# Four feed-forwards of an encoder: one ring for the weight sums, a shifted turn of the operand tiles, and the memory's squares on VectorE

## The chip, the cores and the metric

The kernel runs on one core of a Trainium2 chip. The metric is device time in microseconds (us), from runs on the chip. TensorE (PE in the profile) multiplies matrices, VectorE (DVE), ScalarE (ACT) and GpSimd (POOL) work element by element, and SyncE (SP) issues most DMAs. A DMA that adds to what lies at its destination is issued by POOL here ("accumulate").

## The reference

A two-layer encoder over 512 tokens of 1024 features, in float32. Each layer has a feed-forward, a mixer (attention), a cross attention to a memory of 256 tokens, and a second feed-forward:

```python
def rmsnorm(x, g):
    xf = x.astype(jnp.float32)
    y = xf * lax.rsqrt(jnp.mean(xf * xf, axis=-1, keepdims=True) + EPS)
    return (y * g.astype(jnp.float32)).astype(x.dtype)

def swiglu(x, wg, wu, wd):
    return (jax.nn.silu(x @ wg) * (x @ wu)) @ wd
...
    h = x
    for layer in range(DEPTH):
        g, wg, wu, wd = ffn1[layer]
        h = h + 0.5 * swiglu(rmsnorm(h, g), wg, wu, wd)
        mix_g, mix_params = mix[layer]
        if layer % 2 == 0:
            h = h + even_mixer(rmsnorm(h, mix_g), *mix_params, t5_bias, layer)
        else:
            h = h + odd_mixer(rmsnorm(h, mix_g), *mix_params)
        mg, sg, wq, wkv, qg, kg, wo = memx[layer]
        h = h + memory_xattn(rmsnorm(h, mg), rmsnorm(mem, sg), wq, wkv, qg, kg, wo)
        g, wg, wu, wd = ffn2[layer]
        h = h + 0.5 * swiglu(rmsnorm(h, g), wg, wu, wd)
```

The hidden width of a feed-forward is 2816, 22 blocks of 128.

## The kernel before, in words

The change touches the four feed-forwards, which run at about 0 to 348, 719 to 1038, 1038 to 1367 and 1697 to 2030 us of the profiled execution. Between them stand the mixers and the cross attentions.

**Split products.** A float32 matrix product is made of three products of rounded parts: each operand is split into a high part (ScalarE copies it, rounded) and a low part (VectorE subtracts the high part from it), and high x high, low x high and high x low are added in PSUM. `operand` (L541 high, L542 low) does this for weights. One "product" of a pair is 24 matmuls of 128x256 (18 in the first chunk of the down projection).

**Pairs.** The 22 hidden blocks go in eleven pairs. Pair 0 is plain (`plain_pair`, `plain_end`: there R, the tokens' norm factor, is transposed by TensorE at L418 and copied by VectorE at L419). Pairs 1 to 10 use seven products of quarters instead of eight, in Strassen's manner. For pair p, TensorE's order is: sum t1 and sum t2 (`sum_pair`), cross with w12 and cross t3 (`cross_pair`), then the opening product of pair p+1 with its w11 (`open_pair`), then lower and upper of pair p (`close_pair`). A weight quarter is fetched by SP (`fetch`, L550) into a tile; quarters that have to be added are added by POOL's accumulate. Two tiles hold such sums:

- s1 (in `sum_pair`): SP fetches a quarter, POOL accumulates another on top (L601); t1 multiplies it. Then VectorE subtracts w11 from it in place (L607), t2 multiplies that; last, `close_pair` replaces it by w12 minus it (L655), for upper. So s1 lives through a whole pair. Three buffers.
- s3 (in `cross_pair`): SP fetches a quarter, ScalarE negates it (L632), POOL accumulates another on top (L633); t3 multiplies it. One buffer.

Every operand's high and low parts go into a ring of two tiles (wh, wl), and each third time into tiles of their own (sh, sl); a counter f.n in `operand` decides the turn. The last block of the down projection (L835) also writes its weights into sh and sl.

**Down projection.** The hidden blocks go down in chunks of 6, 8 and 8 blocks. The first two go by seven products as well (`paired_down`, after pairs 3 and 7), with its own s1 (accumulate L760) and s3 (L778) from the same buffers; the last is plain.

**Memory.** In the first feed-forward, `mem_stats` also loads the eight blocks of the memory (128x256) in two lots of four, at pairs 2 and 3. ScalarE squares them, and GpSimd adds the squares (L260), at pairs 3 and 4; at pair 6 the norm factors are made of the sum.

**Order.** PE's order is the one in which the code is written. On the other engines a scheduler in the framework sets the order of instructions when the kernel is built, by its own estimates, by priorities (`high_priority`) and by the order demanded with `behind`; each engine then runs its list strictly in order, and so do SP's and POOL's DMA issues. `f.factored` is the copy of pair 0's norm factor on VectorE (L405).

Of the kernel before, what the change touches and what calls it, by code (L numbers as in the profile page):

```python
# [11 lines left out]
F32 = mybir.dt.float32  # L12
# [7 lines left out]
P = 128  # L20
S = 512
D = 1024
F = 2816
KB = D // P
FB = F // P
QB = S // P
NMEM = 256
# [43 lines left out]
CHUNKS = (6, 8, 8)  # L71
# [3 lines left out]

MEM_SQUARES, MEM_FACTOR = (3, 4), 6
LAMBDA_INIT = 0.8 - 0.6 * math.exp(0.0)
# [35 lines left out]
class Encoder:  # L113
# [205 lines left out]
    def ffn(self, pre):  # L319


        with ExitStack() as ctx:
            pool = lambda name: ctx.enter_context(self.tc.tile_pool(name=pre + name, bufs=1))
            f = self.f = SimpleNamespace(pre=pre, ctx=ctx, hp=pool("h"), tp=pool("t"), H={}, n=0, taken=None, own=False, low=None, gate=None, ahead=None, spread=None, macc=None,
                                        G=[])
# [5 lines left out]
            for p in range(1, FB // 2):  # L331
# [17 lines left out]
                else:  # L349
# [4 lines left out]
                    else:  # L354
                        gate()
                    if c in PAIRED and p == ends[c]:
                        self.paired_down(c)
                        c += 1
# [169 lines left out]

    def operand(self, t, own=None):

        nc, f = self.nc, self.f
        n = t.shape[-1]
        if own is None:
            own = f.n % 3 == 2
            f.n += 1
        if own:
            h, l = (x[:, :n] for x in self.own_tiles())
        else:
            h, l = [self.wp.tile([P, 1024 + WHOLE], F32R, name=name, tag=name, bufs=2)[:, o:o + n]
                    for name, o in (("wh", LINE), ("wl", LINE + STEP))]  # L540
        self.leading = nc.scalar.activation(h, t, AF.Copy)  # L541
        self.parted = nc.vector.tensor_sub(l, t, h.bitcast(F32))  # L542
        return h, l
# [50 lines left out]
    def sum_pair(self, pair):  # L594
# [3 lines left out]
        with self.tc.high_priority():  # L598
            pair.s = f.tp.tile([P, 1024], F32, name="s1", tag="s1", bufs=3)
            self.fetch(pair.s, p, 3, f.first)  # L600
            nc.gpsimd.dma_start(pair.s, self.quarter(p, 2), accum_op=OP.add)  # L601
            w = self.operand(pair.s)
        with self.tc.high_priority():
# [12 lines left out]
    def cross_pair(self, pair):  # L616
# [11 lines left out]
        with self.tc.high_priority():  # L628
            s = f.tp.tile([P, 1024], F32, name="s3", tag="s3", bufs=1)
            self.fetch(s, p, 2)  # L630
# [104 lines left out]
    def paired_down(self, c):  # L735
# [11 lines left out]
        for s in range(2):  # L747
# [9 lines left out]
            with self.tc.high_priority():  # L757
                t = f.tp.tile([P, 1024], F32, name="s1", tag="s1", bufs=3)[:, :n]
                self.fetch(t, p, 3)
# [14 lines left out]
            with self.tc.high_priority():  # L774
                v = f.tp.tile([P, 1024], F32, name="s3", tag="s3", bufs=1)[:, :n]
                self.fetch(v, p, 2)
# [647 lines left out]
    def mem_keys(self, pre, mp):  # L1424
# [14 lines left out]
        return kh, kl, vp  # L1439

    def mem_stats(self, p):

        nc, f = self.nc, self.f
        if p in MEM_SQUARES:
            with self.behind(self.leading):
                for m in f.mem:
                    f.macc = self.square(f.macc, m, NMEM)
        if p + 1 in MEM_SQUARES:
            n = KB // len(MEM_SQUARES)
            f.mem, loaded = [], self.loaded  # L1450
            for k in range(MEM_SQUARES.index(p + 1) * n, MEM_SQUARES.index(p + 1) * n + n):
                if k % 2 == 0:
                    two = f.hp.tile([P, S], F32, name="mem", tag="T", bufs=max(CHUNKS))
                m = two[:, k % 2 * NMEM:k % 2 * NMEM + NMEM]
                with self.behind(loaded):
                    nc.sync.dma_start(m, self.I["memT"][k * P:(k + 1) * P, :])
                f.mem.append(m)
        if p == MEM_FACTOR:
# [448 lines left out]
```

## Time and profile before

| what | value |
|---|---|
| median of three runs | 2031.19 us (2030.74 to 2033.74) |
| the profiled execution | 2032.02 us |
| its span, first to last instruction | 2030.2 us |
| TensorE's mean granted clock | 0.998 |
| busy: PE, DVE, ACT, POOL | 2008.5, 1597.6, 1278.1, 357.0 us |
| HBM read | 301.64 MB |

The profile names a group of instructions by line, engine, operation and tiles (out<-in). A helper records many operations, so one line such as L542 or L565 stands for all operands and all products. "Idle before" is the time in which the engine waited directly ahead of an instruction, with what ended the wait. Since PE is busy in nearly the whole span, the entries that count are those of its idle time.

### The profile page before, as it was taken

How to read it: one execution, taken by the hardware profiler on the slowest of the kernel's cores; microseconds unless marked ns; L12 is line 12 of the kernel's file. 1: busy time of each engine (PE TensorE's matmuls, PEld its weight loads, DVE VectorE, ACT ScalarE, POOL GpSimd, SP SyncE). 2: the span in 40 equal slices, each digit the busy share in tenths (PEclk: the TensorE clock that was granted, in tenths of full speed). 3: DMA queues.
4: the chain of work that ended last, by engine and by line, in shares of the span. 5: the costliest groups of instructions: out<-in, count | busy, mean ns of one | idle time of the engine just before them, and what ended most of it. 6: DMA issues, size and time to landing. Idle time of an engine off the chain costs nothing.

```text
span 2030.2 us, 35251 instructions
## 1 busy us (share of the span) xinstructions
PE 2008.5 (99%) x13849; PEld 1843.1 (91%) x13853; DVE 1597.6 (79%) x2363; ACT 1278.1 (63%) x1955; POOL 357.0 (18%) x339
## 2 busy tenths in 40 slices
PE   9999999999999999999999999999999999999999
PEld 7999998888888899999989999988888888999997
DVE  8979776699676798888679797864668788979784
ACT  7667564656786576665657665745768566766572
POOL 1021001356531111100010101003353111010100
PEclk9999999999999999999999999999999999999999
DMA  7777755322241277776467777544224324777763
GB/s 233 199 200 190 192 164 167 99 79 84 95 139 61 65 235 187 209 189 183 144 177 206 207 187 188 176 140 140 94 84 125 104 73 141 221 209 193 183 177 98
DMA packets 102263, 316.53 MB, mean 156 GB/s; under 512 B 11472, under 2 KB 14672, under 8 KB 102096
## 3 DMA queue, kind: packets, MB, share of 16 engines
q1 hardware_dynamic: 85680, 257.12, 38.6%
q0 software_dynamic: 16128, 56.63, 16.1%
q8 instruction: 109, 1.79, 0.3%
q14 instruction: 58, 0.48, 0.1%
q10 hardware_dynamic: 288, 0.52, 0.1%
HBM read 301.64 MB, written 12.58 MB: 155 GB/s over the span
## 4 chain that ended last, share of the span: by engine, by line
PE 93%; DVE 2%; ACT 2%; DMA 2%; issue 1%; POOL 0%; SPq 0%; DVEq 0%; ACTq 0%; POOLq 0%
PE ps_pa L565 35%; PE ps_pb L565 13%; PE ps_pa L958 13%; PE ps_pa L904 5%; PE ps_pa L835 4%; PE ps_pb L835 4%; PE ps_pb L1071 3%; PE ps_pa L399 2%; PE ps_pa L1561 2%; PE ps_pa L1392 2%; PE ps_pb L1124 1%; PE ps_pb L904 1%; PE ps_pb L1097 1%; PE ps_pa L1291 1%; PE ps_pb L399 1%; DMA s<-l_ffn_wq 1%
## 5 line engine op out<-in xcount | busy, mean ns | idle before, releaser
L169 ACT ACTIVATE wh<-wf 128x1024 fp32r<-128x1024 f32 (+1 forms) x155 | 154.4, 1002 | 178.7 <-issue 37.8
L541 ACT ACTIVATE wh<-s 128x1024 fp32r<-128x1024 f32 (+1 forms) x164 | 168.8, 1029 | 134.6 <-PE ps_pa L565 30.0
L542 DVE TENSOR_TENSOR wl<-s,wh 128x1024 fp32r<-128x1024 f32 (+1 forms) x164 | 193.6, 1182 | 57.9 <-ACT wh L541 55.7
L171 DVE TENSOR_TENSOR wl<-wf,wh 128x1024 fp32r<-128x1024 f32 (+1 forms) x110 | 128.9, 1177 | 43.1 <-ACT wh L169 39.8
L541 ACT ACTIVATE wh<-wf 128x1024 fp32r<-128x1024 f32 (+1 forms) x100 | 103.3, 1033 | 65.4 <-PE ps_pa L565 46.3
L171 POOL TENSOR_TENSOR wl<-wf,wh 128x1024 fp32r<-128x1024 f32 (+1 forms) x45 | 100.0, 2221 | 205.3 <-ACT wh L169 143.1
L542 DVE TENSOR_TENSOR wl<-wf,wh 128x1024 fp32r<-128x1024 f32 (+1 forms) x100 | 118.3, 1186 | 9.9 <-ACT wh L541 9.8
L633 POOL DMA_DIRECT2D s<-l_ffn_wq x40 | 35.1, 879 | 510.3 <-ACT s L632 234.7
L958 PE MATMUL ps_pa<-wh,xh 128*128 128x512 f32 x384 | 121.7, 398 | 0.0
L958 PE MATMUL ps_pa<-wh,xl 128*128 128x512 f32 x384 | 118.8, 391 | 0.0
L958 PE MATMUL ps_pa<-wl,xh 128*128 128x512 f32 x384 | 118.7, 390 | 0.0
L542 DVE TENSOR_TENSOR sl<-wf,sh 128x1024 fp32r<-128x1024 f32 (+1 forms) x68 | 80.3, 1180 | 19.8 <-ACT sh L541 19.8
L541 ACT ACTIVATE sh<-wf 128x1024 fp32r<-128x1024 f32 (+1 forms) x68 | 69.3, 1020 | 34.8 <-PE ps_pa L565 19.3
L958 PEld LDWEIGHTS ps_pa<-wh,xl 128*128 128x128 f32 x384 | 72.1, 188 | 15.7
L958 PEld LDWEIGHTS ps_pa<-wl,xh 128*128 128x128 f32 x384 | 72.0, 188 | 15.6
L542 DVE TENSOR_TENSOR sl<-s,sh 128x1024 fp32r<-128x1024 f32 (+1 forms) x60 | 71.1, 1185 | 17.9 <-ACT sh L541 17.8
L541 ACT ACTIVATE sh<-s 128x1024 fp32r<-128x1024 f32 (+1 forms) x60 | 62.0, 1033 | 36.7 <-PE ps_pb L565 12.9
L1086 ACT ACTIVATE e<-e,m 128x128 f32<-128x128 f32 (+3 forms) x128 | 70.7, 554 | 21.7 <-DVE m L1085 21.5
L958 PEld LDWEIGHTS ps_pa<-wh,xh 128*128 128x128 f32 x384 | 69.2, 188 | 12.3
L601 POOL DMA_DIRECT2D s<-l_ffn_wq x40 | 37.0, 932 | 236.6 <-DMA s<-l_ffn_wq 106.5
L565 PE MATMUL ps_pa<-xh,wh 128*128 128x256 f32 x472 | 73.6, 277 | 0.0
L565 PE MATMUL ps_pa<-xl,wh 128*128 128x256 f32 x472 | 73.1, 276 | 0.0
(460 smaller groups left out, 6204.1 us busy)
## 6 DMA issues: line engine op xcount, KB each, us to landing
wf<-l_ffn_wq SPq DMA_DIRECT2D x120, 512.0 KB, 4.5
s<-l_ffn_wq SPq DMA_DIRECT2D x80, 512.0 KB, 4.4
s<-l_ffn_wq POOLq DMA_DIRECT2D x80, 512.0 KB, 7.9
wf<-l_w_in SPq DMA_DIRECT2D x48, 512.0 KB, 3.4
wf<-l_ffn_wd SPq DMA_DIRECT2D x32, 512.0 KB, 3.7
wf<-l_ffn_wdq SPq DMA_DIRECT2D x24, 512.0 KB, 4.8
wf<-l_ffn_wdq SPq DMA_DIRECT2D x24, 384.0 KB, 3.7
s<-l_ffn_wdq SPq DMA_DIRECT2D x16, 512.0 KB, 3.8
```

Source lines behind the costliest of these rows:

```text
L169: self.leading = nc.scalar.activation(wh[:, sl], w[:, sl], AF.Copy)
L171: eng.tensor_sub(wl[:, sl], w[:, sl], wh.bitcast(F32)[:, sl])
L399: nc.tensor.matmul(p, w[a][:, k * P:(k + 1) * P], xs[k][c], start=k == order[0] and a == c == 0, stop=k == order[-1] and a == 1)
L541: self.leading = nc.scalar.activation(h, t, AF.Copy)
L542: self.parted = nc.vector.tensor_sub(l, t, h.bitcast(F32))
L565: self.nc.tensor.matmul(bank[:, z * 256:z * 256 + 256], w[a][:, o:o + P], xs[k][b], start=first and n == 0, stop=n == len(ops) - 1, skip_g ...
L835: self.nc.tensor.matmul(bank, w[a][:, j * P:(j + 1) * P], h, start=j == a == e == 0 and c < len(CHUNKS) - 1, stop=j == nb - 1 and (a, e) = ...
L904: nc.tensor.matmul(banks[dd], w[g, k // 2][a][:, o:o + P], parts(k)[b], start=k == first and a == b == 0, stop=k == last and a == 1)
L958: nc.tensor.matmul(banks[j], xs[k][a][:, j * P:(j + 1) * P], w[b][:, kk * 512:kk * 512 + 512], start=k == a == b == 0, stop=k == KB - 1 an ...
L1071: nc.tensor.matmul(bank[:, o:o + n], a, b[:, :n], start=c == 0, stop=c == len(ops) - 1)
L1086: nc.scalar.activation(e, e, AF.Exp, bias=m[:, i:i + 1], scale=-1.0, accum_out=rs[:, i:i + 1])
L1392: nc.tensor.matmul(banks[c][i], a[:, i * P:(i + 1) * P], b[:, c * 512:(c + 1) * 512], start=(k == 0 and n == 0), stop=(k == KB - 1 and n = ...
```

## The change

Four edits: s3 takes its buffer from s1's ring, which now has four buffers in place of three and one; the counter of the operands' turn starts at two instead of zero in each feed-forward; the low part of t1 in pair 1 has to come after `f.factored`; and the memory's eight blocks are all loaded at pair 2 into free tiles of the hidden parts, and their squares are added by VectorE just ahead of the first paired chunk.

```diff
--- before.py
+++ after.py
@@ -73,7 +73,7 @@
 
 WARM = 11
 
-MEM_SQUARES, MEM_FACTOR = (3, 4), 6
+MEM_FETCH, MEM_FACTOR = 2, 6
 LAMBDA_INIT = 0.8 - 0.6 * math.exp(0.0)
 
 L0_CHUNKS = [[(2120, 256), (2632, 256)], [(3144, 512)], [(2376, 256), (2888, 256)],
@@ -321,7 +321,7 @@
 
         with ExitStack() as ctx:
             pool = lambda name: ctx.enter_context(self.tc.tile_pool(name=pre + name, bufs=1))
-            f = self.f = SimpleNamespace(pre=pre, ctx=ctx, hp=pool("h"), tp=pool("t"), H={}, n=0, taken=None, own=False, low=None, gate=None, ahead=None, spread=None, macc=None,
+            f = self.f = SimpleNamespace(pre=pre, ctx=ctx, hp=pool("h"), tp=pool("t"), H={}, n=2, taken=None, own=False, low=None, gate=None, ahead=None, spread=None, macc=None,
                                         G=[])
             R = self.plain_pair()
             ends = [sum(CHUNKS[:c + 1]) // 2 for c in range(len(CHUNKS))]
@@ -354,6 +354,8 @@
                     else:
                         gate()
                     if c in PAIRED and p == ends[c]:
+                        if self.mem_r is None and c == 0:
+                            self.mem_squares()
                         self.paired_down(c)
                         c += 1
                 if self.mem_r is None:
@@ -526,7 +528,7 @@
         f.own = True
         return tiles
 
-    def operand(self, t, own=None):
+    def operand(self, t, own=None, after=None):
 
         nc, f = self.nc, self.f
         n = t.shape[-1]
@@ -539,7 +541,8 @@
             h, l = [self.wp.tile([P, 1024 + WHOLE], F32R, name=name, tag=name, bufs=2)[:, o:o + n]
                     for name, o in (("wh", LINE), ("wl", LINE + STEP))]
         self.leading = nc.scalar.activation(h, t, AF.Copy)
-        self.parted = nc.vector.tensor_sub(l, t, h.bitcast(F32))
+        with self.behind(after):
+            self.parted = nc.vector.tensor_sub(l, t, h.bitcast(F32))
         return h, l
 
     def quarter(self, p, q):
@@ -596,10 +599,10 @@
         nc, f, p = self.nc, self.f, pair.p
         pair.z = self.bank("pb")
         with self.tc.high_priority():
-            pair.s = f.tp.tile([P, 1024], F32, name="s1", tag="s1", bufs=3)
+            pair.s = f.tp.tile([P, 1024], F32, name="s1", tag="s1", bufs=4)
             self.fetch(pair.s, p, 3, f.first)
             nc.gpsimd.dma_start(pair.s, self.quarter(p, 2), accum_op=OP.add)
-            w = self.operand(pair.s)
+            w = self.operand(pair.s, None, f.factored if p == 1 else None)
         with self.tc.high_priority():
             xs = self.tokens("1")
         self.product(pair.z, w, xs, True)
@@ -626,7 +629,7 @@
         else:
             nc.scalar.copy(c, self.halves(x))
         with self.tc.high_priority():
-            s = f.tp.tile([P, 1024], F32, name="s3", tag="s3", bufs=1)
+            s = f.tp.tile([P, 1024], F32, name="s3", tag="s1", bufs=4)
             self.fetch(s, p, 2)
             with self.behind(f.led), self.behind(f.taken):
                 nc.scalar.activation(s, s, AF.Copy, scale=-1.0)
@@ -755,7 +758,7 @@
             nc.scalar.copy(x, y)
             z = self.bank("pb")
             with self.tc.high_priority():
-                t = f.tp.tile([P, 1024], F32, name="s1", tag="s1", bufs=3)[:, :n]
+                t = f.tp.tile([P, 1024], F32, name="s1", tag="s1", bufs=4)[:, :n]
                 self.fetch(t, p, 3)
                 nc.gpsimd.dma_start(t, self.quarter(p, 2), accum_op=OP.add)
                 w = self.operand(t)
@@ -772,7 +775,7 @@
             self.product(x, w, f.G["21"], False)
             add(s, 0, 0, x, True)
             with self.tc.high_priority():
-                v = f.tp.tile([P, 1024], F32, name="s3", tag="s3", bufs=1)[:, :n]
+                v = f.tp.tile([P, 1024], F32, name="s3", tag="s1", bufs=4)[:, :n]
                 self.fetch(v, p, 2)
                 nc.scalar.activation(v, v, AF.Copy, scale=-1.0)
                 nc.gpsimd.dma_start(v, self.quarter(p, 0), accum_op=OP.add)
@@ -1438,23 +1441,23 @@
             nc.vector.scalar_tensor_tensor(kl[:, sl], p, gcol, kh.bitcast(F32)[:, sl], op0=OP.mult, op1=OP.subtract)
         return kh, kl, vp
 
+    def mem_squares(self):
+
+        with self.behind(self.leading):
+            for m in self.f.mem:
+                self.f.macc = self.square(self.f.macc, m, NMEM, self.nc.vector)
+
     def mem_stats(self, p):
 
         nc, f = self.nc, self.f
-        if p in MEM_SQUARES:
-            with self.behind(self.leading):
-                for m in f.mem:
-                    f.macc = self.square(f.macc, m, NMEM)
-        if p + 1 in MEM_SQUARES:
-            n = KB // len(MEM_SQUARES)
-            f.mem, loaded = [], self.loaded
-            for k in range(MEM_SQUARES.index(p + 1) * n, MEM_SQUARES.index(p + 1) * n + n):
-                if k % 2 == 0:
-                    two = f.hp.tile([P, S], F32, name="mem", tag="T", bufs=max(CHUNKS))
-                m = two[:, k % 2 * NMEM:k % 2 * NMEM + NMEM]
+        if p == MEM_FETCH:
+            rooms = [f.hp.tile([P, 1024], F32, name="mem", tag="H", bufs=max(CHUNKS))]
+            rooms += [f.hp.tile([P, S], F32, name="mem", tag="T", bufs=max(CHUNKS)) for _ in range(2)]
+            f.mem = [t[:, o:o + NMEM] for t in rooms for o in range(0, t.shape[-1], NMEM)]
+            loaded = self.loaded
+            for k, m in enumerate(f.mem):
                 with self.behind(loaded):
                     nc.sync.dma_start(m, self.I["memT"][k * P:(k + 1) * P, :])
-                f.mem.append(m)
         if p == MEM_FACTOR:
             v, r = self.stats(f.macc, 2)
             self.mem_r = self.const.tile([P, 2], F32, name="mem_r")
```

PE's order is the same but for the tiles that the operands use. The other engines' lists come out in another order. Three places:

POOL, the second feed-forward, around pairs 5 and 6. L601 (now L604) is the accumulate of s1, L633 (now L636) that of s3; the numbers are buffers. Before, in order, these are s1 of pair 5, s3 of pair 4, s1 of 6, s3 of 5, s1 of 7, s3 of 6:

```order
L601 DMA s_9471<-l_ffn_wq 128x1024
L633 DMA s_9322<-l_ffn_wq 128x1024
L601 DMA s_9712<-l_ffn_wq 128x1024
L633 DMA s_9563<-l_ffn_wq 128x1024
L601 DMA s_9953<-l_ffn_wq 128x1024
L633 DMA s_9804<-l_ffn_wq 128x1024
```

And now, from s3 of pair 4:

```order
L636 DMA s_9321<-l_ffn_wq 128x1024
L604 DMA s_9470<-l_ffn_wq 128x1024
L604 DMA s_9711<-l_ffn_wq 128x1024
L636 DMA s_9562<-l_ffn_wq 128x1024
L604 DMA s_9952<-l_ffn_wq 128x1024
L636 DMA s_9803<-l_ffn_wq 128x1024
```

The accumulate of s3 of a pair stood behind that of the next pair's s1 in both lists, but the tile s_9711 (s1 of pair 6) takes over the buffer of s1 of pair 4, whereas s_9712 took one of an earlier use, and s_9953 (s1 of pair 7) the one of pair 4.

VectorE, the first pair of the first feed-forward. s_399 (now s_402) is s1 of pair 1, s_503 its s3; before:

```order
L542 TENSOR_TENSOR wl<-s_399,wh 128x1024
L405 COPY factor<-r 128x4
L607 TENSOR_TENSOR s_399<-s_399,wf 128x1024
L483 TENSOR_TENSOR t2l<-tq,t2h 128x1024
L419 COPY R<-ps_pb 128x512
L542 TENSOR_TENSOR sl<-s_399,sh 128x1024
L542 TENSOR_TENSOR wl<-wf,wh 128x1024
L422 TENSOR_TENSOR gs<-ps_pa,R 128x512 x2
L483 TENSOR_TENSOR t3l<-tq,t3h 128x1024
```

And now:

```order
L407 COPY factor<-r 128x4
L545 TENSOR_TENSOR wl<-s_402,wh 128x1024
L421 COPY R<-ps_pb 128x512
L610 TENSOR_TENSOR s_402<-s_402,wf 128x1024
L485 TENSOR_TENSOR t2l<-tq,t2h 128x1024
L424 TENSOR_TENSOR gs<-ps_pa,R 128x512 x2
L485 TENSOR_TENSOR t3l<-tq,t3h 128x1024
L545 TENSOR_TENSOR wl<-s_402,wh 128x1024
```

The copy of the factor moved ahead of t1's low part, R moved ahead of the subtraction for t2 (L610), and t2's low part, the last row, moved behind both multiplications by R and behind t3l.

SP, the second feed-forward, where the loads of its first pair are issued (s tiles, w11 and w12 as wf) and the tokens' features are put aside (kept). Before:

```order
L550 DMA s_8612<-l_ffn_wq 128x1024
L550 DMA wf<-l_ffn_wq 128x1024 x3
L550 DMA s_8469<-l_ffn_wq 128x1024
L802 DMA kept<-x 128x512 x4
L550 DMA wf<-l_ffn_wq 128x1024
L802 DMA kept<-x 128x512 x4
```

And now:

```order
L553 DMA s_8468<-l_ffn_wq 128x1024
L805 DMA kept<-x 128x512 x5
L553 DMA wf<-l_ffn_wq 128x1024
L805 DMA kept<-x 128x512 x3
L553 DMA wf<-l_ffn_wq 128x1024 x2
L553 DMA s_8611<-l_ffn_wq 128x1024
```

Five of the eight stores of x moved ahead of the first of the three wf loads, w12 of pair 1, and the third pair's s1 (s_8612, now s_8611) moved behind all of these.

## The prediction

> **What bounds the kernel now.** I read the page's busy shares first, then the 40 slices, the releasers of TensorE's idle time, and around single waits the timeline. Of the page:
>
> ```profile
> PE 2008.5 (99%) x13849; PEld 1843.1 (91%) x13853; DVE 1597.6 (79%) x2363; ACT 1278.1 (63%) x1955; POOL 357.0 (18%) x339
> ```
>
> PE is busy 99% of 2030.2 us. The change alters no matmul, so it can only shorten or lengthen PE's idle time. Who ends that idle time, over the whole span:
>
> ```profile
> PE ps_pa L565 <- DVE wl L542: 3.0, 5, 0.7
> PE ps_pa L835 <- ACT sh L169: 2.8, 4, 0.7
> PE ps_pa L565 <- DVE sl L542: 2.6, 4, 0.7
> PE ps_pa L565 <- ACT gu L614: 2.6, 1, 2.6
> PE ps_pa L565 <- ACT wh L541: 0.7, 1, 0.7
> ```
>
> The columns are total us, times, longest. Operands that are late by under a microsecond cost 9.1 us in 14 places, and one wait of 2.6 us stands alone. That one and its neighbourhood, in the timeline of the first feed-forward (start, duration, engine, line; in brackets the idle time before and its releaser):
>
> ```profile
> 114.83 0.33 SPq L550 DMA_DIRECT2D s<-l_ffn_wq  x1
> 119.86 0.88 POOL L601 DMA_DIRECT2D s<-l_ffn_wq  x1 [1.60 <-DMA s<-l_ffn_wq]
> 120.45 1.18 POOL L633 DMA_DIRECT2D s<-l_ffn_wq  x1
> 121.01 2.40 POOL L260 TENSOR_TENSOR acc<-acc,sq 128x256 f32<-128x256 f32 x1
> 121.11 1.72 DVE L607 TENSOR_TENSOR s<-s,wf 128x1024 f32<-128x1024 f32 x1
> 125.70 0.74 PE L565 MATMUL ps_pa<-t2h,wl 128*128 128x256 f32 x4 [0.52 <-DVE wl L542]
> ...
> 129.66 1.06 ACT L541 ACTIVATE wh<-s 128x1024 fp32r<-128x1024 f32 x1 [5.73 <-DMA s<-l_ffn_wq]
> ...
> 132.52 0.56 ACT L614 COPY gu<-ps_pa 128x512 f32<-128x512 f32 x1
> 133.14 0.39 PE L565 MATMUL ps_pa<-t3h,wh 128*128 128x256 f32 x1 [2.55 <-ACT gu L614]
> ```
>
> The chain reads: SP fetches the weights of a later pair's sum s1 at 114.83; POOL's accumulate for it (L601) waits for the landing and starts 5.0 us later; the accumulate for cross's s3 (L633) stands behind it in POOL's queue, at +5.6; it lands at 129.66; ScalarE splits s3, and in its own queue behind that stand a gate, the next w11 and the copy L614, which frees the PSUM bank that t3 writes. TensorE starts t3 at 133.14. From SP's fetch to t3 it took 18.3 us. The granted clock around it:
>
> ```profile
> 131.20:134.60 3.40, 1.46 (x12) 1.47 (x13) 3.40 (x5) 3.32 (x5) 0.00 (x0) 1.00 0.40 125
> 134.60:138.00 3.40, 3.40 (x18) 3.40 (x18) 2.17 (x4) 1.38 (x3) 0.00 (x0) 0.50 0.41 129
> ```
>
> The last four columns end with PEclk, DMA share and GB/s: after the 2.55 us wait the clock was 0.50 for one window, 18 matmul records instead of about 31, so the wait cost another 3.4 x 0.5 = 1.7 us.
>
> **Gains.** (1) Memory's squares: the added L260 leave POOL, so DVE's L607 at 121.11 is no longer stretched to 1.72 us beside L260's 2.40 (1.23 at 34.70, a row below), and the accumulates at 120 change places: -0.5 at 125.70, -2.6 at 133.14, -1.7 of clock, 4.8 in all. DVE takes seven adds of 128x256 instead; DVE's three-operand work on 256 columns takes 0.4 us, so 2.8 us in the paired chunk. They cost nothing on the path as long as that chunk leaves DVE gaps; a row of such a chunk has 0.4 us idle before it. If the cover goes, 2.8 us.
>
> ```profile
> 795.55 0.96 DVE L542 TENSOR_TENSOR wl<-s,wh 128x768 fp32r<-128x768 f32 x1 [0.40 <-ACT wh L541]
> 835.64 0.42 DVE L700 TENSOR_TENSOR t<-gs,t 128x256 f32<-128x256 f32 x1
> ```
>
> (2) Operand count shifted by two: before, the own tile sh is last used by cross's t3 of pair 10, directly ahead of L835, whose loads wait 0.7 us in each feed-forward; now t2 of that pair has it, two products earlier: -2.8. (3) In pairs 4 and 7 VectorE's order brings some low parts ahead of a gate (L688): of wl and wh the remaining 3.0 - 0.5 + 0.7 = 3.2 go. The 2.6 on sl, pair 5's t2, keep their order and stay. Gains: 4.8 + 2.8 + 3.2 = 10.8; with all listed waits and the clock, 11.7 + 1.7 = 13.4, as the upper end.
>
> **Loss 1: the first pair's t2.** Before, VectorE around it:
>
> ```profile
> 34.70 1.23 DVE L607 TENSOR_TENSOR s<-s,wf 128x1024 f32<-128x1024 f32 x1
> 36.98 0.68 DVE L419 COPY R<-ps_pb 128x512 f32<-128x512 f32 x1
> 37.58 1.21 DVE L542 TENSOR_TENSOR sl<-s,sh 128x1024 fp32r<-128x1024 f32 x1
> 34.81 0.65 PE L418 MATMUL ps_pb<-ident,factor 128*128 128x128 f32 x4
> 38.99 0.62 PE L565 MATMUL ps_pa<-t2h,sl 128*128 128x256 f32 x4
> ```
>
> The difference L607 and t2l stood before R, and sl directly behind R. Now R stands ahead of the difference, and behind it come the difference, t2l, two multiplications by R, t3l, and only then t2's low part. R cannot start before the transposes end at 35.4 (34.81 + 0.65). From there: R 0.6 (36.98 to 37.58), difference, t2l and t3l 1.15 each (34.70 to 36.98 for two), twice 0.6, low part 1.2 = 6.4, so 41.8, where TensorE wanted it at 38.99: 2.8 us. The second feed-forward and the fourth have that order too (the third has not): 3 x 2.8 = 8.4. Lower bound 0, if the scheduled order leaves something earlier than I read; upper 3 x 3.4.
>
> There also five stores of x (256 KB each) now go out ahead of w12's load, and one load of s less (512 KB): 0.75 MB more in front, in a stretch where the DMA engines are full:
>
> ```profile
> 727.00:732.00 5.00, 5.00 (x26) 4.17 (x25) 4.97 (x12) 3.15 (x4) 2.00 (x3) 1.00 1.06 294
> ```
>
> At 294 GB/s that is 2.6 us later for w12. ScalarE has w12's split ahead of t2's high part, so it shows, but mostly beside the 2.8 above: I take 1.0 each in the second and fourth, 2.0 (0 to 5). Memory's eight loads (128 KB each) all go out at pair 2 of the first feed-forward instead of in two lots; at the same 294 GB/s 1 MB is 3.6 us of DMA; none of TensorE's waits listed above ends with a load, so I take 0, at most 3.6.
>
> **Loss 2: s3 behind the next sum.** In a ring of four shared by s1 and s3, s1 of pair p+2 takes the buffer of s1 of pair p, which comes free only when the upper product's low part of pair p is written (before, with three for s1 alone, that of pair p+3 took it). POOL's order has the accumulate of s1(p+2) ahead of that of s3(p+1) for p+1 = 2, 5, 6, and likewise a paired chunk's sum ahead of s3 for 3 and 7. So POOL waits for a fetch that starts at R, the end of that low part. In the second feed-forward SP's fetches that waited for just such a low part give R (769.39, 835.75, 856.20, 874.74; for pair 2, 752.26 is the low part's end), and t3's starts give what is wanted:
>
> ```profile
> 751.04 1.22 DVE L542 TENSOR_TENSOR wl<-s,wh 128x1024 fp32r<-128x1024 f32 x1
> 769.39 0.33 SPq L550 DMA_DIRECT2D s<-l_ffn_wdq  x1
> 835.75 0.33 SPq L550 DMA_DIRECT2D s<-l_ffn_wq  x1
> 856.20 0.33 SPq L550 DMA_DIRECT2D s<-l_ffn_wdq  x1
> 874.74 0.33 SPq L550 DMA_DIRECT2D s<-l_ffn_wdq  x1
> 836.19 0.86 POOL L633 DMA_DIRECT2D s<-l_ffn_wq  x1 [13.63 <-DVE t L700]
> 840.37 0.86 POOL L601 DMA_DIRECT2D s<-l_ffn_wq  x1 [3.31 <-DVE xl L715]
> 764.07 0.50 PE L565 MATMUL ps_pa<-t3h,sh 128*128 128x256 f32 x3
> 783.11 0.39 PE L565 MATMUL ps_pa<-t3h,wh 128*128 128x256 f32 x2
> 850.88 0.39 PE L565 MATMUL ps_pa<-t3h,wh 128*128 128x256 f32 x2
> L565 PE MATMUL ps_pa<-t3h,sh x8: 276/276/276, 869.9 to 871.6; 128*128 128x256 f32 x8
> L565 PE MATMUL ps_pa<-t3h,wh x8: 276/276/276, 889.9 to 891.6; 128*128 128x256 f32 x8
> DMA to landing us min/median/max: 5.3/6.9/11.9
> ```
>
> The two POOL rows show what changes: before, s3's accumulate was issued at 836.19 and a sum's at 840.37, after its fetch of 835.75 had landed; now the s3 one stands behind it. The last row is L633's landing. The chain from R to t3, by the rows of the first feed-forward: 5.6 to the issue, 6.9 (median) to the landing, 3.5 (129.66 to 133.14) to t3 = 16.0. So t3 is late by 769.39 + 16.0 - 783.11 = 2.3, 835.75 + 16.0 - 850.88 = 0.9, 2.3 at 869.9, 0.8 at 889.9, and in pair 2, where no gate stands behind the split (1 us less), 752.26 + 15.0 - 764.07 = 3.2: 9.5 us a feed-forward. With the shortest landing, 5.3, the same sum is 1.6 + 0.7 + 0 + 0.7 + 0 = 3.0; with the 18.3 measured once, 5.5 + 4.6 + 3.2 + 4.6 + 3.1 = 21. I take 7.5, between the median and the shortest and nearer to the median, because this order keeps fewer fetches in flight, so 4 x 7.5 = 30 (12 to 84; below nothing only if s3's earlier fetch helped, but TensorE waited for s3 at one place only, and that is counted above).
>
> **Loss 3: the clock.** Three waits of 2.8 us or more in the first pairs and four of about 3 at pair 2 resemble the 2.55 us one. A window fits over a wait only by chance; I count half of seven, 3.5 x 1.7 = 6 (0 to 12).
> The Trainium skill, "TensorE: Matmul & The Clock Gate", Part 1 (What's actually happening), has the clock halved only after at least one idle window of about 3.4 us on a free-running grid; by that rule none of these waits would count, and the sum would be 6 us lower. The rows above differ from it: 1.46 us of matmuls in the window did not prevent the half clock.
>
> **Sum.** 2032.0 (this execution; 2030.2 of span) - 10.8 + 8.4 + 2.0 + 30 + 6 = 2067.6; the median of the runs is 0.8 below this execution, so 2066.8; I say 2067.
>
> **Rivals.**
> Hidden: the accumulate lands in about 5 us, so s3 is no later than TensorE. Then Loss 2 and most of the clock go: 2031.2 - 10.8 + 8.4 + 2 = 2030.8, within 0.2% (4.1 us, about what a measurement of this kernel can tell). For it speaks that the shortest landing is 5.3 and that loss falls by 1 us for each us of landing at five places; against it the median of 6.9.
> The Trainium skill, "DMA: Bandwidth & Descriptors", Anatomy of one DMA (SWDGE path), fits such a transfer as 2.0 us plus bytes over 436e3 per us, for 512 KB an estimate of 3.2 us, which would put it here; the landing row does not agree, its shortest is 5.3.
> Faster: the same, and all listed waits gone with the low part of t2 late by half of what I worked out: 2031.2 - 13.4 + 4.2 = 2022. It decides where the landing stays under 5 us and t2's low part is late by under 1.4 us a pair. 13 in 100.
> Worse: landings like the 9.1 us one (120.45 to 129.6), the second of two accumulates issued 0.6 us apart, as every one of these now is: 84 instead of 30, and all the clock windows: 2031.2 - 10.8 + 10.4 + 84 + 12 = 2127. More likely half way, 2095.
> The ring without effect: if POOL's wait costs nothing because s3's own scaling is later, the first pair alone counts; that is the time of Hidden.
>
> **How the numbers follow.** Forecast 0.58 (2045 to 2085), worse 0.21, hidden 0.08, faster 0.13. Leaving out the worst and the best, 2026 to 2095. Slower 0.79, same 0.08, faster 0.13.
>
> **What would show it.** Right: TensorE's waits on L565 by ScalarE's gu copy and wh in about five places of each feed-forward, together over 15 us; one wait of 2 to 3 us on wl at 39 to 42, 740 and 1725; no more wait at L835; PEclk under 0.9 in some slices. Wrong: t3 starting on time in pairs 2 and 6 (then POOL's wait is hidden), L601 waiting for no DMA before s3's L633, or t2's low part in time in the first pair.

## The result, and the profile after

| | median, us | range, us | against before (95% interval) |
|---|---|---|---|
| before | 2032.47 | 2030.74 to 2035.36 | |
| changed | 2048.50 | 2046.92 to 2053.28 | 1.0081 (1.0060 to 1.0103) |

The change made the kernel 16 us slower, 0.8%. The forecast had 35 us slower: the sign was right and the size twice too large, and that it is off by no more hides two errors: the largest term of the sum did not come at all, and a small one came several times larger. The profiled execution took 2048.73 us, 16.7 more than that of before. The four feed-forwards, from their first matmul to their last product in the timeline, took -2.2, +9.7, +1.5 and +7.8 us against before; the stages between them are unchanged.

The engines' busy times, and below them the largest of TensorE's waits by what ended them (total us, times, longest), over the whole span of the changed kernel:

```profile
PE 2010.5 (98%) x13853; PEld 1844.7 (90%) x13853; DVE 1596.8 (78%) x2370; ACT 1275.6 (62%) x1955; POOL 350.7 (17%) x332
PE ps_pa L568 <- ACT gu L591: 17.1, 4, 7.3
PE ps_pa L568 <- ACT ps_pa L758: 3.5, 4, 1.2
PE ps_pa L568 <- DVE wl L545: 3.5, 5, 0.9
PE ps_pa L568 <- ACT wh L543: 1.7, 2, 1.2
PE ps_pa L568 <- ACT sh L543: 1.5, 1, 1.5
```

L568 is the products' line, L565 before. The wait at the last down block (2.8 us before) is gone, and so is the 2.6 us one on gu L614 (memory's squares). In their place stands gu L591, 17.1 us in four places. L591 copies the opening product out of PSUM ahead of t2, so all four are the first pair's t2, one for each feed-forward. The second feed-forward's, in the timeline of the changed kernel:

```profile
718.38 4.79 SPq L805 DMA_DIRECT2D kept<-x  x5
724.08 1.06 ACT L635 ACTIVATE s<-s 128x1024 f32<-128x1024 f32 x1 [0.15 <-DMA s<-l_ffn_wq]
724.12 0.33 SPq L553 DMA_DIRECT2D wf<-l_ffn_wq  x1
...
740.71 1.06 ACT L543 ACTIVATE sh<-wf 128x1024 fp32r<-128x1024 f32 x1 [8.35 <-DMA wf<-l_ffn_wq]
741.67 1.04 ACT L482 ACTIVATE t4h<-tq 128x1024 fp32r<-128x1024 f32 x1
742.62 1.04 ACT L543 ACTIVATE wh<-s 128x1024 fp32r<-128x1024 f32 x1
743.56 0.56 ACT L591 COPY gu<-ps_pa 128x512 f32<-128x512 f32 x1
744.18 0.80 PE L568 MATMUL ps_pa<-t2h,wh 128*128 128x256 f32 x2 [7.34 <-ACT gu L591]
744.10:747.50 3.40, 3.32 (x15) 3.32 (x16) 3.40 (x4) 3.32 (x4) 0.00 (x0) 0.50 0.01 4
```

Read from the bottom: TensorE stood 7.34 us, and the window after it (last row) ran at half clock. It waited for the last of four ScalarE instructions in a row, of which the first is the split of w12, and that one had waited 8.35 us for w12 to land. w12's load was issued at 724.12, behind the five stores of x, and landed 16.5 us later. What t2 needs of the other engines had long been there: VectorE had the difference that t2 multiplies with done at 735.97, and the low part of its tokens at 737.10. Only ScalarE's own pieces, the difference's high part (wh) and the copy, were held up behind w12's split.

The issue itself was late too. SP's loads and stores in this program count on eight semaphores in turn: in the trace the instruction ahead of w12's load waits on semaphore 108, which the load itself counts on, and which was last used by s3's first quarter, fetched at 716.95 and landed at 724.06. So w12 is issued as the transfer eight places ahead of it lands, and the stores take up places. Before, w12's load was issued at 722.85 and landed 12.4 us later. Here it was issued 3.4 us later, measured from the start of the feed-forward, and was 4.1 us longer on its way: 7.5 us in all.

### The profile page after: what moved, and what is told of

The parts are those of the page before. It is cut to its first block, busy times and chain, and to the rows that moved or that the text cites. A ratio compares the mean times of both kernels' runs of the same rounds, so it can differ in the third digit from the quotient of the medians.

```text
span 2046.7 us, 35261 instructions
## 1 busy us (share of the span) xinstructions
PE 2010.5 (98%) x13853; PEld 1844.7 (90%) x13853; DVE 1596.8 (78%) x2370; ACT 1275.6 (62%) x1955; POOL 350.7 (17%) x332
## 4 chain that ended last, share of the span: by engine, by line
PE 83%; DMA 6%; DVE 6%; ACT 3%; issue 2%; SPq 0%; POOL 0%; ACTq 0%; DVEq 0%; POOLq 0%
PE ps_pa L568 30%; PE ps_pa L961 13%; PE ps_pb L568 10%; PE ps_pa L907 5%; PE ps_pa L838 4%; PE ps_pb L838 4%; PE ps_pb L1074 3%; DMA s<-l_ffn_wdq 2%; DMA wf<-l_ffn_wq 2%; PE ps_pa L1564 2%; PE ps_pa L1395 2%; PE ps_pb L1127 1%; PE ps_pb L1100 1%; DVE wl L545 1%; PE ps_pb L907 1%
## 5 line engine op out<-in xcount | busy, mean ns | idle before, releaser
L169 ACT ACTIVATE wh<-wf 128x1024 fp32r<-128x1024 f32 (+1 forms) x155 | 154.6, 1003 | 175.2 <-issue 37.6
L543 ACT ACTIVATE wh<-s 128x1024 fp32r<-128x1024 f32 (+1 forms) x132 | 136.5, 1035 | 129.2 <-DMA s<-l_ffn_wq 34.7
L545 DVE TENSOR_TENSOR wl<-s,wh 128x1024 fp32r<-128x1024 f32 (+1 forms) x132 | 157.0, 1190 | 74.4 <-ACT wh L543 74.1
L545 DVE TENSOR_TENSOR wl<-wf,wh 128x1024 fp32r<-128x1024 f32 (+1 forms) x132 | 154.6, 1171 | 24.5 <-ACT wh L543 24.2
L543 ACT ACTIVATE wh<-wf 128x1024 fp32r<-128x1024 f32 (+1 forms) x132 | 134.4, 1018 | 61.1 <-PE ps_pa L568 50.1
L171 DVE TENSOR_TENSOR wl<-wf,wh 128x1024 fp32r<-128x1024 f32 (+1 forms) x110 | 128.7, 1175 | 42.0 <-ACT wh L169 40.0
L604 POOL DMA_DIRECT2D s<-l_ffn_wq x40 | 35.9, 897 | 583.0 <-DMA s<-l_ffn_wq 217.5
L545 DVE TENSOR_TENSOR sl<-s,sh 128x1024 fp32r<-128x1024 f32 (+1 forms) x92 | 108.1, 1175 | 30.4 <-ACT sh L543 30.1
L543 ACT ACTIVATE sh<-s 128x1024 fp32r<-128x1024 f32 (+1 forms) x92 | 94.1, 1023 | 46.7 <-PE ps_pa L568 35.5
L568 PE MATMUL ps_pa<-xh,wh 128*128 128x256 f32 x560 | 86.9, 276 | 0.0
L568 PE MATMUL ps_pa<-xl,wh 128*128 128x256 f32 x560 | 86.9, 276 | 0.0
L568 PE MATMUL ps_pa<-xh,wl 128*128 128x256 f32 x560 | 86.9, 276 | 0.0
L568 PEld LDWEIGHTS ps_pa<-xh,wh 128*128 128x128 f32 x560 | 74.2, 188 | 0.0
L568 PEld LDWEIGHTS ps_pa<-xh,wl 128*128 128x128 f32 x560 | 74.2, 188 | 0.0
```

The costliest lines, as they stand in the source:

```text
L169: self.leading = nc.scalar.activation(wh[:, sl], w[:, sl], AF.Copy)
L171: eng.tensor_sub(wl[:, sl], w[:, sl], wh.bitcast(F32)[:, sl])
L568: self.nc.tensor.matmul(bank[:, z * 256:z * 256 + 256], w[a][:, o:o + P], xs[k][b], start=first and n == 0, stop=n == len(ops) - 1, skip_g ...
```

## The experiments

The experiments ran in four batches after the first result. Medians are in us; each ratio is to the kernel before in the same batch, whose median lay between 2032.4 and 2034.2.

| kernel | median | ratio to before (95%) |
|---|---|---|
| changed | 2048.50 | 1.0081 (1.0060 to 1.0103) |
| ring4_only: before + ring of four | 2065.18 | 1.0167 (1.0147 to 1.0187) |
| no_ring: changed, old buffers | 2027.65 | 0.9970 (0.9959 to 0.9982) |
| early_stores: no_ring + stores ahead of w12 | 2044.68 | 1.0057 (1.0045 to 1.0070) |
| late_store: changed, stores behind pair 2's w12 | 2044.43 | 1.0061 (1.0045 to 1.0076) |
| late_both: late_store + chunk's scaling later | 2069.65 | 1.0176 (1.0156 to 1.0196) |
| ring22: changed, two rings of two | 2042.76 | 1.0045 (1.0032 to 1.0058) |
| rings22_late: ring22 + late stores | 2036.43 | 1.0014 (1.0005 to 1.0024) |
| forced: ring22 + s3 made to follow the next s1 | 2166.26 | 1.0649 (1.0628 to 1.0670) |
| shift_only: before + shifted turn | 2041.33 | 1.0034 (1.0022 to 1.0047) |
| no_fact: changed, t1's low part free | 2051.19 | 1.0093 (1.0079 to 1.0107) |
| r_behind: no_ring, R behind t2's low part | 2031.18 | 0.9988 (0.9979 to 0.9996) |
| mem_only: before + memory's squares | 2027.49 | 0.9971 (0.9960 to 0.9983) |
| mem_last: mem_only + t3 of pair 10 in the ring | 2025.29 | 0.9960 (0.9947 to 0.9974) |

**The ring alone, and the change without it.** ring4_only puts the two buffer lines of the diff on the kernel before; no_ring takes them out of the changed one:

```diff
-            s = f.tp.tile([P, 1024], F32, name="s3", tag="s1", bufs=4)
+            s = f.tp.tile([P, 1024], F32, name="s3", tag="s3", bufs=1)
```

(and three for s1, in all four places).

> The kernel before with the shared ring of four alone (no shifted turn, no constraint on t1's low part, memory's squares as they were). The stores come out ahead of pair 1's w12 as in the changed kernel. Theory A (the ring's stores are the main loss): w12 lands about 7 us later, two waits of 6 to 8 us with half clock in the second and fourth feed-forward, about 17 us more than before, 2046 to 2052 us. Theory B (the loss needs the shifted turn or R's new place too): under 6 us more, 2031 to 2038 us.

> The changed kernel with the buffers as they were before (three for s1, one for s3); the shifted turn, the order of t1's low part and memory's squares stay. Theory A (the ring is the whole loss by way of the stores ahead of w12 and of the paired chunk's s3, and the other three edits bring what was forecast as gains, about 11 us, less about 3 us in each first pair where R stands early): the two long waits go, 2022 to 2030 us. Theory B (the other edits lose too): over 2032 us.

Without the ring the change is 5 us faster than before; the ring costs 20.9 us on it (2048.50 - 2027.65) and 33 us on the kernel before, more than Theory A had for ring4_only. Beside t2 of the first pairs (6.50 us of wait at 746 in the second feed-forward), that kernel's profile has waits of 3.0, 3.6 and 2.1 us, start to start, at t2 of pair 7, and others in the paired chunks. no_ring's releasers show no long wait:

```profile
PE ps_pa L568 <- ACT gu L591: 5.0, 3, 1.7
PE ps_pa L568 <- DVE wl L545: 2.7, 3, 0.9
PE ps_pa L568 <- DVE sl L545: 2.4, 4, 0.6
```

**The stores.** set_aside puts each store behind "the last load issued", which is s3 of pair 2. With one buffer for s3 that load had to wait for pair 1's t3; with four it goes out at once, and the stores with it. late_store and early_stores move only the stores, in opposite directions:

```diff
-                with self.behind(self.loaded):
+                with self.behind(f.crossload):    # late_store: pair 2's w12
...
-                with self.behind(self.loaded):
+                with self.behind(f.sumload):      # early_stores, on no_ring: pair 2's s1
```

> The changed kernel with one edit: the stores that put the features aside are ordered behind pair 2's w12 load instead of behind the last load of s3 that was issued. Theory A (the stores stand in SP's queue ahead of pair 1's w12 and delay it; the four-buffer ring let s3 of pair 2 be fetched at once and so let the stores go early): the two long waits of 7.5 and 7.1 us before t2 in the second and fourth feed-forward and their half clock (together 9.8 and 9.2 us) shrink to what the first feed-forward shows there, about 3 us each; 13 us less, about 2035 us. Theory B (w12 is late because ScalarE comes to its split late, or because of the weight sums' own loads): no change, 2046 to 2050 us. Theory C (the stores only cost somewhere else): under 5 us less.

> The kernel without the ring (three buffers for s1, one for s3, the other three edits in) with one edit: the stores that put the features aside may go out behind the load of pair 2's s1, so that five of eight stand ahead of pair 1's w12, as they do with the ring. Theory A (early stores alone make w12 late, whatever the buffers): waits of 7 to 9 us ahead of t2 of pair 1 in the second and fourth feed-forward, 10 to 14 us more than the 2027.65 us without the ring, 2037 to 2042 us. Theory B (the ring's other loads made w12 late): under 4 us more.

early_stores took 17.0 us more than no_ring. Its w12 and t2 in the second feed-forward; the fourth has the same wait. With the half clock behind it, t2 lost 11.7 and 11.9 us there, from start to start:

```profile
721.63 0.33 SPq L553 DMA_DIRECT2D wf<-l_ffn_wq  x1
739.96 1.06 ACT L543 ACTIVATE sh<-wf 128x1024 fp32r<-128x1024 f32 x1 [10.22 <-DMA wf<-l_ffn_wq]
743.43 0.79 PE L568 MATMUL ps_pa<-t2h,wh 128*128 128x256 f32 x2 [8.92 <-ACT gu L591]
```

So early stores make w12 late with the old buffers too: that is shown, and the time is above Theory A's 2037 to 2042. The reverse came out smaller than expected, 4 us instead of 13, and the intervals of late_store and of the changed kernel overlap. In late_store the long waits did go (gu L591 from 17.1 to 5.0 us in total), but other waits grew. Its releasers, in a profiled execution that was the slowest of its six (2052.15):

```profile
PE ps_pa L568 <- ACT ps_pa L759: 6.9, 6, 1.3
PE ps_pa L568 <- ACT wh L543: 6.4, 5, 2.3
PE ps_pa L568 <- DVE wl L545: 5.3, 7, 0.9
PE ps_pa L568 <- ACT gu L591: 5.0, 3, 1.7
```

The first two lines are the paired chunks, and pairs 3 and 7. The largest of them are t2 of pairs 3 and 7 in the second feed-forward; at pair 3:

```profile
785.43 0.84 ACT L781 ACTIVATE s<-s 128x768 f32<-128x768 f32 x1 [4.85 <-DMA s<-l_ffn_wdq]
787.76 0.74 PE L568 MATMUL ps_pa<-t2h,wh 128*128 128x256 f32 x4 [1.92 <-ACT wh L543]
```

ScalarE stands 4.85 us at the scaling of the next chunk's s3 (L781 here, L780 in the other kernels), which its list has ahead of the splits for t2. At pair 7 the changed kernel has the same place: ScalarE stood 4.27 us, t2 waited 1.21. no_ring has that scaling behind t2's split, and no such wait. These waits are the ring's, then. They also differ from one execution to the next: late_store's first feed-forward, which has no stores and in which every engine has the order of the changed kernel's, took 6.3 us longer in its profile than there (340.7 against 334.5). The six executions of late_store spread over 12 us, those of no_ring over 3.6. Early stores alone cost 17.0 us without the ring, and the ring with late stores still costs 16.8 (2044.43 - 2027.65), while both together cost 20.9: each is enough to lose most of it, and the two do not add up.

**The chain of s3.** ring22 was meant to bring about the late s3 of the forecast; forced does:

```diff
+                f.pref = self.prefetch(p + 1) if not final and p >= 2 and p not in ends else None
                 self.cross_pair(pair)
...
-            nc.gpsimd.dma_start(s, self.quarter(p, 0), accum_op=OP.add)
+            with self.behind(f.pref and f.pref[2]):
+                nc.gpsimd.dma_start(s, self.quarter(p, 0), accum_op=OP.add)
```

prefetch issues the fetch and the accumulate of the next pair's s1.

> The changed kernel with the four buffers cut in two rings, two for s1 and two for s3, so that s1 of pair p+2 must take the buffer of s1 of pair p; POOL's order stays word for word. Theory A (the forecast's late s3 failed because in the shared ring s1 of pair p+2 took the buffer of s3 of pair p, free some 6 us earlier, and the chain of 16 us itself is right): t3 becomes late in several pairs of each feed-forward, 3 to 9 us in each, 2060 to 2085 us. Theory B (the chain is hidden whatever buffer is taken, since the shifted turn lets the upper product's parts be made earlier): 2046 to 2052 us.

> The changed kernel with two rings of two, in which, for pairs 2, 4, 5, 6, 8 and 9, the fetch and the accumulate of the next pair's s1 are written ahead of the cross products and the accumulate of s3 must follow that of s1; s1's buffer is that of the pair before last. (The run with two rings of two alone did not have this order: POOL's list there has s3's accumulate first in nearly all pairs, so it did not test the chain as its expectation said.) Theory A (the forecast's chain is right where its two conditions hold): t3 late by 1 to 4 us in most of these 24 places, 25 to 70 us more than the 2042.8 us of two rings alone. Theory B (the chain of 16 us is too long or t3 has more room than worked out): under 10 us more.

In ring22 neither theory was tested, because its expectation had POOL's order wrong: with s1's buffer freed later, the scheduler put s3's accumulate first (L636 is s3's, L604 s1's):

```profile
841.72 0.86 POOL L636 DMA_DIRECT2D s<-l_ffn_wq  x1 [13.90 <-ACT s L635]
846.09 0.86 POOL L604 DMA_DIRECT2D s<-l_ffn_wq  x1 [3.51 <-DVE xl L718]
```

forced has both conditions, and took 123.5 us more than ring22. Its t3 waits 80.2 us in 21 places, and the clock adds to it (mean granted clock 0.973). One place, and the releaser's row:

```profile
860.57 0.33 SPq L554 DMA_DIRECT2D s<-l_ffn_wq  x1
866.37 0.86 POOL L603 DMA_DIRECT2D s<-l_ffn_wq  x1 [14.56 <-DVE x L760]
866.90 1.22 POOL L648 DMA_DIRECT2D s<-l_ffn_wq  x1
876.25 1.06 ACT L544 ACTIVATE sh<-s 128x1024 fp32r<-128x1024 f32 x1 [6.72 <-DMA s<-l_ffn_wq]
879.11 0.56 ACT L628 COPY gu<-ps_pa 128x512 f32<-128x512 f32 x1
879.73 0.56 PE L569 MATMUL ps_pa<-t3h,sh 128*128 128x256 f32 x1 [4.45 <-ACT gu L628]
PE ps_pa L569 <- ACT gu L628: 80.2, 21, 5.8
```

From SP's fetch to t3 it is 19.2 us here, more than the 16.0 and even the 18.3 of the forecast. Its 123.5 us are beyond Theory A's 25 to 70. The chain is real; the changed kernel does not meet its conditions.

**The paired chunks.** In the changed kernel t2 of the first paired chunk waits 0.7 to 1.6 us, start to start, in each feed-forward. In the third:

```profile
1130.51 0.85 ACT L780 ACTIVATE s<-s 128x768 f32<-128x768 f32 x1 [3.49 <-DMA s<-l_ffn_wdq]
1131.26 0.83 ACT L543 ACTIVATE wh<-s 128x768 fp32r<-128x768 f32 x1
1131.99 0.57 ACT L654 COPY gu<-ps_pa 128x512 f32<-128x512 f32 x1
```

ScalarE stands 3.49 us at the scaling of the chunk's s3 (L780), ahead of the split of the chunk's s1 and a copy. late_both orders that scaling behind t2's split, with the stores late; rings22_late has two rings and the stores late.

```diff
-                nc.scalar.activation(v, v, AF.Copy, scale=-1.0)
+                with self.behind(split):
+                    nc.scalar.activation(v, v, AF.Copy, scale=-1.0)
```

> The changed kernel with two edits: the stores behind pair 2's w12, and in the paired chunks the scaling of s3 on ScalarE behind the split of t2's weights. Theory A (the ring's 21 us are the early stores, about 10, and ScalarE's wait for the chunk's s3 ahead of its sum's split, about 10): 2027 to 2034 us. Theory B (waits come back elsewhere, as with the stores alone, 2044.4): 2038 to 2046 us.

> The changed kernel with two rings of two and the stores ordered behind pair 2's w12. Theory A (the early stores are the cause of the two waits of 8.6 and 8.9 us seen with two rings of two too, and nothing else replaces them): 12 to 14 us less than with two rings alone, 2028 to 2032 us. Theory B (as with the shared ring, other late operands take most of it back): 2036 to 2042 us.

late_both was 25 us slower than late_store, beyond both theories: with the scaling later, s3 lands later, and ScalarE stands at its split instead (5.50 us up to 124.04), with t3 of the chunk waiting 2.10 us at 126.14 for the copy behind it. So moving that one instruction does not settle how much L780's place costs. ring22, where such waits of over 0.7 us do not appear in the second and fourth feed-forward, is 5.7 us under the changed kernel, with intervals that just do not overlap. rings22_late gave 6.3 us of the 12 to 14 expected: the long waits went, waits on the copy L642 (7.3 us, 8 times) came.

**R's place in the first pair, and the shift.**

> The changed kernel without the demand that t1's low part in pair 1 comes after the norm factor; on VectorE, R's copy then falls behind the low parts of t2 and w12 in the first pair. Theory A (R ahead of t2's parts costs 3.1 us in the first and 1.4 us in the third feed-forward, and in the second and fourth hides behind the late w12): 4 to 5 us less, 2043 to 2045 us. Theory B (R later only moves the wait to the gates and t3): 2046 to 2050 us.

> The kernel before with the operands' turn shifted by two alone. Theory A (the wait at the last down block goes, 3.9 us with refill, and some low parts come earlier): 2024 to 2029 us. Theory B (the shift pushes R behind later low parts in the first pair, so gates and t3 come late there, and the gain is used up): 2030 to 2036 us.

> The kernel without the ring, with R's copy and what needs it on VectorE ordered behind the low part of t2 in pair 1. Theory A (R ahead of t2's parts costs about 3 us in the first, second and fourth feed-forward, and nothing needs R soon): 2018 to 2022 us. Theory B (t3's low part and the gates, now last, make t3 or the next pair late instead): 2025 to 2034 us.

The shift alone costs 8 us. That is a loss, as Theory B had it, but above its 2030 to 2036 and in another place: VectorE has the subtraction for t2 ahead of the factor, so TensorE's transposes wait (9.0 us in three places, and 5.0 more on gu L614). With the factor first and R early (no_ring), t2 waits; with R behind t2's low part (r_behind), w12's product waits as well. The rows are from the second feed-forward of shift_only, the second of no_ring and the first of r_behind:

```profile
744.85 1.12 PE L418 MATMUL ps_pb<-ident,factor 128*128 128x128 f32 x4 [4.46 <-DVE factor L405]
```

```profile
736.93 0.73 PE L568 MATMUL ps_pa<-t2h,wh 128*128 128x256 f32 x4 [1.69 <-ACT gu L591]
739.02 0.74 PE L568 MATMUL ps_pa<-t2h,wl 128*128 128x256 f32 x4 [0.90 <-DVE wl L545]
```

```profile
45.12 0.74 PE L573 MATMUL ps_pa<-xh,sh 128*128 128x256 f32 x4 [2.51 <-DVE gs L429]
```

R's place moves most of a wait of about 2.5 us from one product to another, and r_behind still has 4.0 us at t2 (on the copy, L596 there) beside the 7.5 at w12's product; it is 3.5 us slower than no_ring. So R ahead of the difference is not the only reason why t2 is late. Whether the constraint on t1's low part is what the shift needs is not shown: without it the changed kernel is 2.7 us slower, with intervals that overlap, but no_ring, which has it, has none of shift_only's waits at the transposes.

**The gains alone.**

```diff
-            w = self.operand(s)
+            w = self.operand(s, False if p == FB // 2 - 1 else None)   # mem_last, on mem_only
```

> The kernel before with memory's squares moved alone (loads at pair 2, seven adds on VectorE ahead of the first paired chunk). Theory A (the wait of 2.6 us before t3 of pair 4, its half clock and the 0.5 us wait go; the seven adds are hidden): 5 us less, 2026 to 2029 us. Theory B (the adds delay the paired chunk's parts by as much as they free): 2030 to 2034 us.

> The kernel before with memory's squares moved and one more edit: t3 of pair 10 takes the ring's tiles instead of the own ones, so that the last down block may fill its own tiles two products earlier; the turn is not shifted anywhere else. Theory A (the wait at the last block, 0.97 us from start to start in each of four feed-forwards, is worth what it shows and goes with nothing in its place): 3 to 4 us less than the 2027.5 us of memory's squares alone, 2023.5 to 2024.5 us, and no wait at the last block's line. Theory B (t3 of pair 10 then waits for its ring tile by as much): 2026.5 to 2028.5 us.

Memory's squares alone are worth 5.0 to 5.5 us, as expected. mem_last is 2.2 us below mem_only, less than expected, and measured in another batch, with ratios whose intervals overlap; the wait at the last block, 2.8 us in mem_only, is gone from its releasers, while gu L640 rose from 0.3 to 1.1 us. It is the fastest kernel here, 0.4% under before.

## Why the forecast was wrong

**Loss 2, the late s3 (30 us): did not happen.** This is the step that failed. It took the ring of four to hand out its buffers in turn, so that s1 of pair 6 takes that of s1 of pair 4, free with the upper product's low part. In the changed kernel's timeline it doesn't:

```profile
836.34 1.22 DVE L545 TENSOR_TENSOR sl<-s,sh 128x1024 fp32r<-128x1024 f32 x1
837.59 0.33 SPq L553 DMA_DIRECT2D s<-l_ffn_wq  x1
842.33 1.23 DVE L545 TENSOR_TENSOR sl<-s,sh 128x1024 fp32r<-128x1024 f32 x1 [0.23 <-ACT sh L543]
843.58 0.33 SPq L553 DMA_DIRECT2D s<-l_ffn_wq  x1
842.51 0.86 POOL L604 DMA_DIRECT2D s<-l_ffn_wq  x1 [14.39 <-DVE t L703]
844.02 0.86 POOL L636 DMA_DIRECT2D s<-l_ffn_wq  x1 [0.65 <-ACT s L635]
852.74 1.06 ACT L543 ACTIVATE wh<-s 128x1024 fp32r<-128x1024 f32 x1 [1.30 <-DMA s<-l_ffn_wq]
858.73 0.62 PE L568 MATMUL ps_pa<-t3h,wh 128*128 128x256 f32 x4
```

The first low part (836.34, done at 837.56) is that of t3 of pair 4, the second (done at 843.56) that of upper. The fetch of s1 of pair 6, for which POOL's L604 waits, follows the first, so it takes s3's buffer, 6 us earlier; the fetch behind the second is s3's of pair 6. POOL comes to s3's accumulate of pair 5 at 844.02, when its scaling has just ended (its releaser is L635), and s3 is split 6 us before t3 starts, with no wait. With the fetch 6 us earlier, the forecast's own sum gives no lateness here, and TensorE's releasers name no wait at t3 in any pair. So the step that failed is the path: the fetch that POOL waits for doesn't start at the upper product's low part (R of the forecast), and the 30 us measured nothing. The statement ahead of the forecast that s_9711 takes the buffer of s1 of pair 4 is the same mistake. The price of the chain, where it exists, was too low if anything: 19.2 us in forced against 16.0.

**Loss 1: t2 (8.4 us) right, w12 (2.0 us) mis-sized.** The first pair's t2 waited 1.66 and 0.90 us in the first feed-forward, 2.6 against 2.8; no_ring has 1.69 and 0.90 in the second too, and 7.7 in all over the same three feed-forwards. The size was right, but it comes as two waits, the larger on ScalarE's copy L591, where the forecast had one on the low part. w12 was priced at 2.6 us of bytes, mostly beside t2's wait. Its split ran at 740.71, in a feed-forward that began 2.2 us earlier than before, where it ran at

```profile
735.65 1.04 ACT L541 ACTIVATE wh<-wf 128x1024 fp32r<-128x1024 f32 x1
```

so w12 was 7.5 us late, and t2 with half clock lost about 9.7 and 9.2 us, start to start, instead of 3.8. early_stores put the price of the early stores at 17 us. The bytes were counted, and so was w12's split ahead of t2's high part on ScalarE. Not counted were that the stores also delay w12's issue, that w12 is 4.1 us longer on its way and not 2.6, and that the copy L591 stands in the same queue. A w12 that is 7.5 us late can't hide beside a wait of 2.8.

**Gains (10.8 us): about right.** Memory's squares gave 5.0 to 5.5 (4.8 forecast). The last block's wait (2.8) is gone, of which mem_last shows 2.2 in the time of the whole kernel. The waits on wl and wh (3.2 forecast) are gone as well: what the releasers name under wl L545 now are the first pairs' and those of pair 5, which the forecast kept. In no_ring the gains by waits are then about 10 us; its first pairs' t2 takes back 7.7, and a half clock behind it in the fourth feed-forward about 2.9. That leaves next to nothing, while no_ring is 5 us under before: where the rest comes from is open.

**Loss 3, the clock (6 us): size near, by luck.** The changed kernel ran at half clock in two stretches of 6.8 us, both beginning within the 7 us waits; by their matmuls they cost about 4.4 us (an estimate: half of the 4.6 and 4.2 us that these took). The waits that the forecast's count rests on did not bring it: those at pair 2 did not come, and the 1.66 and 0.90 us in the first feed-forward's first pair left the clock at full:

```profile
39.80:43.20 3.40, 3.06 (x26) 3.07 (x27) 3.40 (x4) 1.93 (x3) 0.00 (x0) 1.00 0.00 0
```

The same two waits in no_ring's fourth feed-forward were followed by two windows at half clock:

```profile
1723.58 1.22 PE L568 MATMUL ps_pa<-t2h,wl 128*128 128x256 f32 x4 [0.90 <-DVE wl L545]
1722.70:1726.10 3.40, 2.52 (x12) 2.53 (x13) 3.40 (x4) 1.09 (x2) 0.00 (x0) 0.51 0.10 41
```

So waits of this size bring it in some places and not in others, as the forecast had it ("only by chance").

**The sign of being right.** The forecast looked for waits on gu copy and wh of together over 15 us, in about five places of each feed-forward. The changed kernel has 17.1 on the gu copy and 1.7 on wh, but the 17.1 stand in four places, at t2 of the first pairs: the number was met by another mechanism.

**The rivals.** "Hidden" had the right mechanism (s3 in time) with the wrong cause, an accumulate that lands in 5 us; landings stayed as they were (844.02 to about 852.7 above). Its time, 2030.8, had w12 at 2.0 us like the forecast, and missed it in the same way. Not foreseen: the paired chunks' scaling of s3 on ScalarE. Why moving the stores later returned 4 us where moving them earlier cost 17 is answered in part: with the ring, other waits, at the chunks' scaling above all, take back part of what the late stores save. How the ring's 20.9 us divide among the stores and these waits stays open.

## What to carry to other kernels

A shared ring frees transfers, and whatever is ordered behind "the last load" comes free with them: look at which loads and stores will now stand ahead of the first operand of a stage, and follow that operand through the in-order queue of the engine that splits it. Before pricing a wait for a buffer, establish which buffer is taken, from the order of the last reads and not from the order of the code; a chain of 16 us is worth nothing if its first link starts 6 us earlier. Count the places in front of a load as well as the bytes, where loads and stores share a few semaphores in turn. A bundle of edits is best taken apart: here one edit lost 21 us and hid a version that is 0.3% faster than the kernel before.

## What the runs showed of the hardware

Beside the loads, the stores of x took three times as long to land as in the kernel before, where the median of the same eight is 5.4 us in the second feed-forward (issued from 745 to 750). The issues view of the changed kernel from 715 to 742 us:

```profile
kept<-x SPq DMA_DIRECT2D x8, 256.0 KB, 15.9
```

In that stretch w12's issue at 724.12 comes as s3's first quarter lands (ScalarE takes it at 724.08), and seven issues between 722 and 739 each come within 0.1 us after the landing of the transfer eight places ahead. By the trace this is the program's doing: its eight semaphores, each waited for before its next use. Of the clock: waits of 2.55 us (before), 4.45 us (forced) and 7.34 us were each followed by at least one window near half clock. Waits of 1.7 and 0.9 us were followed by it in the fourth feed-forward of no_ring, and not in its second nor in the first of the changed kernel. The window behind forced's wait:

```profile
879.70:883.00 3.30, 3.27 (x15) 3.28 (x16) 3.27 (x6) 1.40 (x2) 0.00 (x0) 0.51 0.39 151
```
